# Rates and delay of the late modulation sums in a gated two-mixer layer

## The chip, the cores and the metric

The kernel runs on one core of a Trainium2 chip. Its time is the device time of one execution in microseconds. Three runs of the kernel before took 1473.76 to 1475.06 us, with a median of 1474.42 us. All arithmetic is float32: each large product is made of three TensorE products of a high and a low part.

## What is computed

One layer (DEPTH is 1) over 256 latent and 256 context tokens of width 2048. Six modulation vectors come from one conditioning vector. Two of them (sa, ca) shape the first norm; the other four (ga, cm, sm, gm) are not needed before the end of the mixers.

```python
mod = (jax.nn.silu(c) @ w_mod[l] + b_mod[l])[:, None, :]
sa, ca, ga, sm, cm, gm = jnp.split(mod, 6, axis=-1)
h = modulate(x, norm_attn_w[l], sa, ca)
p = h @ w_in[l]
q = axial_rope(rmsnorm(split_qk(p[..., Q_OFF:K_OFF]), q_norm_w[l]), row, col)
k = axial_rope(rmsnorm(split_qk(p[..., K_OFF:V_OFF]), k_norm_w[l]), row, col)
v = split_v(p[..., V_OFF:P_OFF])
mix = token_mixer(q, k_all, v_all, p[..., P_OFF:G_OFF], p[..., G_OFF:], lam, lam_init,
                  subln_w[l], pool_w[l], pool_scale[l], w_a_up[l], w_b_up[l], w_o[l])
x = x + ga * mix
x = x + gm * sq_relu_mlp(modulate(x, norm_mlp_w[l], sm, cm), w_ff1[l], w_ff2[l])
```

`token_mixer` is differential attention over 8 heads, a multi-scale pooling of a projection, sigmoid gates of both, and the projection `w_o`.

## The kernel before

The weights are streamed once, in chunks of 128 x 1024 floats (512 KB), in an order that the list `stream` fixes (L126 to L172). For each chunk SP issues the load into one of five `raw` buffers (L113 to L116), ACT casts it to the rounded high part `whi` (L233), and DVE subtracts to give the low part `wlo` (L234); there are three buffers of either. `load_next` does this, and `wchunk` runs two chunks ahead of their use. In the products of features by weights (`xstat`, L423 to L446) a chunk for two token tiles is eight matmuls with `whi` (L442, L443) and four with `wlo` (L445); for four token tiles it is twice that.

The stages are: the norms and the first keys and queries (ended at about 131 us), values of group 0, queries, keys and values of group 1, the pooling projection, the gates with their up projections (four groups of 24 chunks), `w_o` (four groups of eight chunks), and the feed-forward. Attention runs beside them: its generator is advanced by a count of matmuls. For one unit, TensorE makes two score tiles (L704), DVE their row maxima `mx` (L705), ACT the exponentials `e` (L709), DVE and ACT the difference of the two softmaxes (L712 to L715); later the result is transposed (`aTp`, `aT`). The keys and queries of group 1 are normed on DVE (`qraw`, L457 to L472) and transposed on TensorE (`qkT`, L477). PSUM has eight banks, all from one pool, so a new tile waits until the tile that held its bank was read.

The late modulation is the subject of the change. The products of silu(c) with the weights of ga, cm, sm and gm do not run on TensorE. For each of these vectors, in two halves of 1024 columns, `late_gen` (L599 to L632) clears an accumulator `macc` on POOL (L617), loads the bias into its first row from POOL's queue, and takes 16 chunks of weights: each is one more load into a `raw` buffer and one multiply-add `late_part` on DVE (L636), 128 in all. At the end of a half, `late_half` splits the two quarters of `macc` into `ah` (ACT, L259) and `al` (DVE, L260), and `late_sum` has TensorE add up the partitions with a tile of ones (`late`, L655 and L656), from where ACT or DVE writes the result. There are 16 such pairs of matmuls.

How often a late chunk is asked for is set by the rate in `stream`: each loaded weight chunk adds its rate to a credit, and each whole credit advances `late_gen` by one chunk. `later(n, fn)` puts a step off by n weight chunks: `tick` runs it when TensorE's program takes its n-th next chunk. A late part runs one chunk after its load where the rate is 1 or more, two where it is less; the product of a late sum stands three chunks behind the split. The order in which each engine gets its instructions is then fixed when the program is built, and an engine that waits for one holds all behind it.

One more place is touched without being edited. In `pooling` ACT copies the projection's two halves into `za` (L798), POOL adds up windows of them (L803), and DVE corrects the edges (L814, L816) and subtracts (L818).

The code of these functions:

Of the kernel before, what the change touches and what calls it, by code (L numbers as in the profile page):

```python
# [48 lines left out]
def layer(ctx: ExitStack, tc, a, out):  # L49
# [24 lines left out]
    def work(name, shape=None, dt=F32):  # L74
        return pool.tile(shape or [P, 512], dt, tag="w2", name=name, bufs=9)
# [19 lines left out]
    def later(n, fn):  # L95

        waiting.append([n, fn])
# [28 lines left out]
    def plan(name, *idx, rate=0.0):  # L126
        stream.append(((name,) + idx, rate))
# [12 lines left out]
            plan("w_k", 0, f // 2)  # L140
            plan("w_q", 0, f // 2)
    FIRST_LOADS = len(stream)
    for n, g, rate in (("w_v", 0, 0.75), ("w_q", 1, 1.0), ("w_k", 1, 1.5), ("w_v", 1, 1.5)):
        for ch in range(8):
            plan(n, g, ch, rate=0.0 if (n, g) == ("w_v", 1) and ch < 3 else rate)
    for g in range(4):
# [9 lines left out]
                    plan("pool_w", 2 if ch == 1 else 3)  # L156
    for g in range(4):
        for ch in range(8):
            plan("w_o", g, ch, rate=0.5 if g < 2 else 0.0)
            if ch % 4 == 0:  # L160
                plan("x", ch // 4, g)
    for b in range(9):
# [95 lines left out]
    def split(hi, lo, src):  # L258
        act.copy(hi, src)  # L259
        vec.tensor_sub(lo, src, hi.bitcast(F32))  # L260
# [377 lines left out]
    def late_split(acc, norm_w, o):  # L638
        for q in range(2):
            part = partial(late_half, q, acc, norm_w, o)  # L640
            if q == 0:
                part()
            else:
                later(2, part)
                parts.append(waiting[-1])

    def late_half(q, acc, norm_w, o):
        ah, al = work("ah", dt=F32R), work("al", dt=F32R)
        split(ah, al, acc[:, q * 512:q * 512 + 512])
        later(3, partial(late_sum, ah, al, norm_w[q] if norm_w else None, o[:, q * 512:q * 512 + 512]))  # L650

    def late_sum(ah, al, wr, o):

# [526 lines left out]
```

## Time and profile before

| | |
|---|---|
| median of the three runs | 1474.42 us (1473.76 to 1475.06) |
| the profiled execution | 1475.86 us |
| its span | 1474.0 us |
| TensorE busy | 1440.5 us, 98% |
| VectorE (DVE) busy | 1000.8 us, 68% |
| ScalarE (ACT) busy | 684.3 us, 46% |
| GpSimd (POOL) busy | 121.3 us, 8% |
| mean granted clock of TensorE | 0.99 |
| HBM traffic over the span | 235 GB/s |

The profile is of one execution. Its span goes from the first instruction to the last, 1.86 us less than the execution's time. In a row of the timeline stand the start and the length in us, the engine, the line of the kernel, the operation, what it writes and reads, the shape, and how many alike follow one another; in brackets how long the engine stood idle ahead of it, and what released it. In a row of the table of waits stand who waited for what, the us in total, how many times, and the longest. The clock is the share of full speed that TensorE was granted.

### The profile page before, as it was taken

What the parts mean: (1) busy time and instruction counts of PE and PEld (TensorE: products, weight loads), DVE (VectorE), ACT (ScalarE), POOL (GpSimd) and SP (SyncE); (2) the same over time, 40 slices, a digit from 0 to 9 for tenths busy, and PEclk for the clock granted to TensorE, in tenths of its full rate; (3) what the DMA queues carried; (4) which work ended last, traced back from release to release, by engine and by line L of the source; (5) the groups of instructions that cost most, each with busy time, mean ns of one, the idle gap of its engine ahead of it and who ended that gap; (6) DMA issues with size and microseconds to landing.
All of it is one profiled execution on the core that took longest, in us unless ns stands there. A gap on an engine that the chain in (4) does not pass through costs nothing.

```text
span 1474.0 us, 19772 instructions
## 1 busy us (share of the span) xinstructions
PE 1440.5 (98%) x7466; PEld 1186.7 (81%) x7466; DVE 1000.8 (68%) x1243; ACT 684.3 (46%) x929; POOL 121.3 (8%) x120
## 2 busy tenths in 40 slices
PE   4999999999999999999999999999999999999998
PEld 2667887778878888888878888888888888888887
DVE  4667786768887687778776755666665555555675
ACT  4334346466554444544444555445354454544442
POOL 0001110101400000000001000001000000000260
PEclk7999999999999999999999999999999999999999
DMA  9996685435788879798746776677765655566554
GB/s 380 401 407 224 203 287 167 143 114 165 234 284 294 301 279 301 278 330 294 252 146 222 233 237 226 234 239 240 238 230 186 193 192 189 191 193 191 186 195 141
DMA packets 97440, 347.85 MB, mean 236 GB/s; under 512 B 11073, under 2 KB 11713, under 8 KB 97345
## 3 DMA queue, kind: packets, MB, share of 16 engines
q1 hardware_dynamic: 96768, 345.51, 69.4%
q8 instruction: 58, 0.95, 0.3%
q0 software_dynamic: 576, 1.08, 0.2%
q14 instruction: 38, 0.30, 0.1%
HBM read 344.45 MB, written 2.10 MB: 235 GB/s over the span
## 4 chain that ended last, share of the span: by engine, by line
PE 88%; DVE 6%; ACT 2%; DMA 2%; issue 1%; POOL 0%; DVEq 0%; SPq 0%; ACTq 0%; POOLq 0%
PE f L1029 14%; PE f L443 8%; PE f L442 8%; PE f L445 8%; PE f L1032 7%; PE pg L443 3%; PE pg L442 3%; PE pg L445 3%; PE w_k L67 3%; PE wo L442 2%; PE wo L445 2%; PE wo L443 2%; PE pyy L445 2%; PE pyy L442 2%; PE pyy L443 2%; DVE wlo L234 2%
## 5 line engine op out<-in xcount | busy, mean ns | idle before, releaser
L234 DVE TENSOR_TENSOR wlo<-raw,whi 128x1024 fp32r<-128x1024 f32 (+1 forms) x433 | 538.4, 1245 | 349.1 <-ACT whi L233 324.1
L233 ACT CAST whi<-raw 128x1024 fp32r<-128x1024 f32 (+1 forms) x433 | 452.8, 1047 | 555.6 <-PE f L443 184.6
L1029 PE MATMUL f<-h,whi 128*128 128x512 f32 x896 | 224.3, 392 | 0.0
L443 PE MATMUL f<-whi,act 128*128 128x512 f32 x512 | 199.3, 389 | 0.0
L442 PE MATMUL f<-whi,act 128*128 128x512 f32 x512 | 199.2, 389 | 0.0
L1029 PEld LDWEIGHTS f<-h,whi 128*128 128x128 f32 x896 | 161.8, 189 | 29.6
L636 DVE SCALAR_TENSOR_TENSOR macc<-raw,sil,macc 128x1024 f32<-128x1024 f32 x128 | 165.0, 1289 | 3.3 <-issue 2.6
L445 PE MATMUL f<-wlo,act 128*128 128x512 f32 x512 | 136.8, 389 | 0.0
L1032 PEld LDWEIGHTS f<-h,wlo 128*128 128x128 f32 x896 | 122.2, 190 | 8.7
L1032 PE MATMUL f<-h,wlo 128*128 128x256 f32 x896 | 124.9, 282 | 0.0
L445 PEld LDWEIGHTS f<-wlo,act 128*128 128x128 f32 x512 | 96.1, 188 | 19.9
L443 PEld LDWEIGHTS f<-whi,act 128*128 128x128 f32 x512 | 96.2, 188 | 19.8
L442 PEld LDWEIGHTS f<-whi,act 128*128 128x128 f32 x512 | 96.2, 188 | 19.7
L442 PE MATMUL pg<-whi,hL 128*128 128x512 f32 x256 | 101.4, 396 | 0.0
L443 PE MATMUL pg<-whi,hL 128*128 128x512 f32 x256 | 100.6, 393 | 0.0
L1040 POOL TENSOR_TENSOR rsq<-relu 128x512 f32<-128x512 f32 x28 | 29.2, 1042 | 543.3 <-ACT relu L1039 523.0
L445 PE MATMUL pg<-wlo,hL 128*128 128x512 f32 x256 | 68.6, 390 | 0.0
L443 PEld LDWEIGHTS pg<-whi,hL 128*128 128x128 f32 x256 | 48.5, 189 | 10.4 <-issue 0.2
L442 PEld LDWEIGHTS pg<-whi,hL 128*128 128x128 f32 x256 | 48.5, 189 | 10.3 <-issue 0.2
L445 PEld LDWEIGHTS pg<-wlo,hL 128*128 128x128 f32 x256 | 48.3, 189 | 10.2
L617 POOL MEMSET macc<- 128x1024 f32 x8 | 7.6, 955 | 461.6 <-DVE al L260 357.1
L442 PE MATMUL wo<-whi,mix 128*128 128x512 f32 x116 | 45.2, 390 | 0.0
(263 smaller groups left out, 2083.4 us busy)
## 6 DMA issues: line engine op xcount, KB each, us to landing
raw<-in_w_ff_dram SPq DMA_DIRECT2D x240, 512.0 KB, 4.0
raw<-in_w_m_dram SPq DMA_DIRECT2D x64, 512.0 KB, 9.7
raw<-in_w_ga_dram SPq DMA_DIRECT2D x32, 512.0 KB, 4.6
raw<-in_w_cm_dram SPq DMA_DIRECT2D x32, 512.0 KB, 4.4
raw<-in_w_gb_in_dram SPq DMA_DIRECT2D x32, 512.0 KB, 4.7
raw<-in_w_ga_in_dram SPq DMA_DIRECT2D x32, 512.0 KB, 5.0
raw<-in_w_sm_dram SPq DMA_DIRECT2D x32, 512.0 KB, 4.8
raw<-in_w_o_dram SPq DMA_DIRECT2D x32, 512.0 KB, 5.2
```

The lines of the kernel that those rows point to most:

```text
L67: return (lambda *a, **k: pin(emit(*a, **k))) if self.flag[0] else emit
L233: act.copy(hi, raw)
L234: vec.tensor_sub(lo, raw, hi.bitcast(F32))
L442: pe.matmul(banks[t], tok(h, k, 0, tt), wt, start=k == 0, stop=False)
L443: pe.matmul(banks[t], tok(h, k, 1, tt), wt, start=False, stop=False)
L445: pe.matmul(banks[t], tok(h, k, 0, tt), wt, start=False, stop=k == 2 * nk - 1)
L617: gp.memset(acc, 0.0)
L636: pin(vec.scalar_tensor_tensor(acc, raw, sil[:, 0, k:k + 1], acc, ALU.mult, ALU.add))
L1029: pe.matmul(ps, hi[:, kk * P:kk * P + P], both(h2, k), start=k == 0, stop=False)
L1032: pe.matmul(ps[:, T:2 * T], lo[:, kk * P:kk * P + P], act_slice(h2, k, 0), start=False, stop=k == KT - 1)
L1040: gp.tensor_mul(sq, r, r)
```

## The change

Three numbers are edited. Of the late chunks, fewer are asked for during keys and values of group 1 (one per weight chunk rather than 1.5 in the keys, 0.75 rather than 1.5 in the last five chunks of the values), more during the first two groups of `w_o` (0.75 rather than 0.5). And the product of a late sum stands four chunks behind its split rather than three.

```diff
@@ -140,7 +140,7 @@
-    for n, g, rate in (("w_v", 0, 0.75), ("w_q", 1, 1.0), ("w_k", 1, 1.5), ("w_v", 1, 1.5)):
+    for n, g, rate in (("w_v", 0, 0.75), ("w_q", 1, 1.0), ("w_k", 1, 1.0), ("w_v", 1, 0.75)):
         for ch in range(8):
             plan(n, g, ch, rate=0.0 if (n, g) == ("w_v", 1) and ch < 3 else rate)
@@ -156,7 +156,7 @@
-            plan("w_o", g, ch, rate=0.5 if g < 2 else 0.0)
+            plan("w_o", g, ch, rate=0.75 if g < 2 else 0.0)
@@ -647,7 +647,7 @@
     def late_half(q, acc, norm_w, o):
         ah, al = work("ah", dt=F32R), work("al", dt=F32R)
         split(ah, al, acc[:, q * 512:q * 512 + 512])
-        later(3, partial(late_sum, ah, al, norm_w[q] if norm_w else None, o[:, q * 512:q * 512 + 512]))
+        later(4, partial(late_sum, ah, al, norm_w[q] if norm_w else None, o[:, q * 512:q * 512 + 512]))
```

All 128 late parts and all 16 pairs of matmuls remain. The late chunks of ga, cm and sm are reached later than before, and the four chunks of gm that were taken in `w_o` now come in the feed-forward, at its rate of 0.25. On TensorE nothing but the 16 pairs moves. On the other engines three places change that matter below.

The first is DVE in the values of group 1, where an attention unit is finished and the next one's maxima follow (at 268 to 277 us of the profile before). Before:

```order
L460 TENSOR_TENSOR qraw<-qraw,rq_y 128x512
L712 RECIPROCAL rs<-sm_2346 128x2
L636 SCALAR_TENSOR_TENSOR macc<-raw,sil,macc 128x1024
L472 TENSOR_TENSOR qraw<-qraw,wkt 128x512
L713 TENSOR_TENSOR rs<-rs,nlam 128x1
L234 TENSOR_TENSOR wlo<-raw,whi 128x1024
L715 SCALAR_TENSOR_TENSOR e<-e,rs 128x512
L636 SCALAR_TENSOR_TENSOR macc<-raw,sil,macc 128x1024 x2
L234 TENSOR_TENSOR wlo<-raw,whi 128x1024
L705 TENSOR_REDUCE mx<-sc 128x1 x2
```

DVE at the same place in the changed kernel:

```order
L460 TENSOR_TENSOR qraw<-qraw,rq_y 128x512
L712 RECIPROCAL rs<-sm_2334 128x2
L472 TENSOR_TENSOR qraw<-qraw,wkt 128x512
L713 TENSOR_TENSOR rs<-rs,nlam 128x1
L234 TENSOR_TENSOR wlo<-raw,whi 128x1024
L715 SCALAR_TENSOR_TENSOR e<-e,rs 128x512
L234 TENSOR_TENSOR wlo<-raw,whi 128x1024
L705 TENSOR_REDUCE mx<-sc 128x1 x2
```

The three late parts L636 no longer stand ahead of the maxima; the rest keeps its order.

The second is ACT in the first group of the gates, up to the sigmoids of the second gate (`pg_3988` and `pg_3989` are its banks; at 437 us of the profile before the casts `ah` stand here). Before:

```order
L833 ACTIVATE py<-pd,prm 128x256 x2
L233 CAST whi<-raw 128x1024
L259 CAST yb<-py 128x512
L233 CAST whi<-raw 128x1024 x8
L259 CAST ah<-macc 128x512 x2
L233 CAST whi<-raw 128x1024 x4
L853 ACTIVATE sgm<-pg_3988 128x512
```

ACT there in the changed kernel, where that bank is called `pg_3962`:

```order
L833 ACTIVATE py<-pd,prm 128x256 x2
L233 CAST whi<-raw 128x1024
L259 CAST yb<-py 128x512
L233 CAST whi<-raw 128x1024 x12
L853 ACTIVATE sgm<-pg_3962 128x512
```

The two casts of a late sum left this stretch; they stand behind the first group's gates now, in the second group.

The third is ACT from the last window of the pooling into the gates (384 to 394 us). Before:

```order
L259 CAST dh<-d 128x512
L233 CAST whi<-raw 128x512
L798 COPY za<-pin 128x256
L724 COPY aT<-aTp 128x4x128
L798 COPY za<-pin 128x256
L233 CAST whi<-raw 128x1024
L259 CAST oT<-osb 128x512
L233 CAST whi<-raw 128x1024 x2
L833 ACTIVATE py<-pd,prm 128x256 x2
```

ACT there in the changed kernel:

```order
L259 CAST dh<-d 128x512
L233 CAST whi<-raw 128x512
L724 COPY aT<-aTp 128x4x128
L259 CAST ah<-macc 128x512
L233 CAST whi<-raw 128x1024
L259 CAST oT<-osb 128x512
L798 COPY za<-pin 128x256 x2
L259 CAST ah<-macc 128x512
L233 CAST whi<-raw 128x1024 x2
L833 ACTIVATE py<-pd,prm 128x256 x2
```

The two casts of another late sum (of ga's second half) came into this stretch, and the two copies `za`, on which POOL's additions wait, moved behind one of them, a weight cast and the cast of `oT`.

## The prediction

> **What bounds the kernel now.** I read the busy table of the page first, then the table of waits for TensorE, then windows of the span, and last the timeline around each wait.
>
> ```profile
> PE 1440.5 (98%) x7466; PEld 1186.7 (81%) x7466; DVE 1000.8 (68%) x1243; ACT 684.3 (46%) x929; POOL 121.3 (8%) x120
> PE qkT L477 <- ACT e L709: 2.5, 1, 2.5
> ...
> PE late L655 <- ACT ah L259: 1.1, 1, 1.1
> PE late L656 <- DVE al L260: 0.8, 1, 0.8
> ```
>
> TensorE is busy for 98% of the span: the kernel is bound by its matmuls, and nothing but their count, their clock and TensorE's idle time sets the end. The change leaves the matmuls and their order as they are but for 16 pairs (L655 and L656) that stand elsewhere. So all it can win is idle time of TensorE and the slow clock that follows it. Behind the opening, the table of waits names only a handful of places; the three above are all that the change could touch.
>
> ```profile
> 250.00:300.00 50.00, 47.46 (x214) 36.61 (x214) 34.71 (x62) 24.08 (x48) 4.41 (x3) 0.97 0.43 136
> 400.00:450.00 50.00, 48.09 (x207) 38.91 (x206) 40.97 (x45) 24.13 (x29) 2.55 (x4) 0.97 0.88 292
> 750.00:800.00 50.00, 47.01 (x211) 37.51 (x210) 33.90 (x52) 21.21 (x31) 0.00 (x0) 0.97 0.50 158
> 450.00:500.00 50.00, 50.00 (x226) 41.46 (x226) 39.55 (x38) 22.01 (x24) 0.00 (x0) 1.00 0.87 295
> ```
>
> In these windows (width, busy time of PE, PEld, DVE, ACT, POOL, then granted clock, DMA share, GB/s) three of four lose two to three us of TensorE each and show a clock of 0.97; the fourth is what an undisturbed one looks like. The waits above lie in these three windows; I call them A (250 to 300), B (400 to 450) and C (750 to 800).
>
> **Stall A, second values group: about 4.0 us, and it goes.**
>
> ```profile
> 268.65 1.26 DVE L636 SCALAR_TENSOR_TENSOR macc<-raw,sil,macc 128x1024 f32<-128x1024 f32 x1
> 271.65 1.06 ACT L233 CAST whi<-raw 128x1024 fp32r<-128x1024 f32 x1 [0.25 <-DMA raw<-in_w_v_dram]
> 272.30 2.59 DVE L636 SCALAR_TENSOR_TENSOR macc<-raw,sil,macc 128x1024 f32<-128x1024 f32 x2
> 274.81 1.22 DVE L234 TENSOR_TENSOR wlo<-raw,whi 128x1024 fp32r<-128x1024 f32 x1
> 275.95 1.28 DVE L705 TENSOR_REDUCE mx<-sc 128x1 f32<-128x512 f32 x2
> 276.66 0.69 ACT L709 ACTIVATE e<-sc,mx 128x512 f32<-128x512 f32 x1 [3.96 <-DVE mx L705]
> 277.59 1.09 PE L477 MATMUL qkT<-prm,qraw 128*128 128x128 f32 x4 [2.54 <-ACT e L709]
> ```
>
> Read from the bottom: TensorE stood 2.54 us before qkT, for a bank whose score ACT had still to read; ACT's exponential waited 3.96 us for the row maxima; and these stood on DVE behind two late parts (L636, 2.59 us) and a weight split. Of the three L636 in these rows the change leaves none there, as its DVE order shows. Then the L234 of 274.81 is held only by its cast. If that cast comes as late as now (271.65 + 1.06 = 272.71), split (1.22), first maximum (half of 1.28) and exponential (0.69) end near 275.26; TensorE gets there at 277.59 - 2.54 = 275.05. So at worst about 0.2 to 0.5 us of waiting is left. At best the weights' load comes earlier as well, since no late loads stand ahead of it on SP, and nothing is left. I take nothing left.
>
> ```profile
> 441.13 0.63 PE L443 MATMUL pg<-whi,hL 128*128 128x512 f32 x1
> 441.56 0.63 PE L442 MATMUL pg<-whi,hL 128*128 128x512 f32 x1
> 445.24 0.40 PE L442 MATMUL pg<-whi,hL 128*128 128x512 f32 x1
> 445.47 0.40 PE L443 MATMUL pg<-whi,hL 128*128 128x512 f32 x1
> ```
>
> The second part of the price is the clock. Behind stall B matmuls start 0.43 us apart, later 0.23; the same stretch follows A. It holds some 3.4 us, in which about seven matmuls each cost 0.20 more: near 1.5 us. So A costs 2.54 + 1.5 = **4.0 us**. The Trainium skill, "TensorE: Matmul & The Clock Gate", Part 1 (The HAM clock gate), says that the clock falls to half after at least one idle window of 3.4 us and that the window runs free. Here the slow stretch has that length, but 2.54 us of idleness brought it on (for B, 1.91 in two pieces), so the trace doesn't bear out the threshold; by the rule the 3.0 us that I put down to the two slow stretches would not belong to these waits, and the time would come out by so much higher.
>
> **Stall B, gates: about 3.5 us, and it goes.**
>
> ```profile
> 437.58 1.05 ACT L233 CAST whi<-raw 128x1024 fp32r<-128x1024 f32 x1 [0.90 <-DMA raw<-in_w_ga_in_dram]
> 438.54 1.13 ACT L259 CAST ah<-macc 128x512 fp32r<-128x512 f32 x2
> 439.20 0.50 PE L655 MATMUL late<-ah,ones 128*128 128x512 f32 x1 [1.07 <-ACT ah L259]
> 440.55 0.50 PE L656 MATMUL late<-al,ones 128*128 128x512 f32 x1 [0.84 <-DVE al L260]
> ```
>
> TensorE waits twice in one late sum: for ah, whose cast stands on ACT behind a weight cast that waited for DMA, and for al, which follows ah on DVE: 1.07 + 0.84 + 1.6 of slow clock = **3.5 us**. With one chunk more between the casts and the product, a chunk being 8 matmuls at 0.23 and 4 at 0.22 (2.7 us), each of the waits would be covered. The half also ends elsewhere now: no ah stands on ACT in this stretch.
>
> The other 15 pairs move too. Each costs two matmuls wherever it stands, so nothing in sum. A pair adds a wait only if its ah or al is late: there are 2 us and more between the splits' and the products' places in the changed order, laid on the old times. The edits of the rates move whole parts: one L636 of DVE and one 512 KB load each.
>
> ```profile
> L636 DVE SCALAR_TENSOR_TENSOR macc<-raw,sil,macc 128x1024 f32<-128x1024 f32 x128 | 165.0, 1289 | 3.3 <-issue 2.6 <-DMA macc<-in_b_cm_dram 0.3 <-DVE rs L712 0.2
> L617 POOL MEMSET macc<- 128x1024 f32 x8 | 7.6, 955 | 461.6 <-DVE al L260 357.1 <-DVE lm L67 104.5
> ...
> macc<-in_b_cm_dram POOLq DMA_DIRECT2D x2, 4.0 KB, 3.2
> ```
>
> In the second keys 8 x 0.5 = 4 parts fewer are asked for, in the second values 5 x 0.75 = 3.75, in w_o 16 x 0.25 = 4 more, and the remaining 3.75 come in the feed-forward, at one per four chunks as now. All 128 stay, DVE's total too, so this costs nothing in itself. Each half's MEMSET (0.96) and bias load (3.2 to landing) on POOL's queue move with it, and at one place they matter, below.
>
> **Where it can be given back: from pooling into the gates.**
>
> ```profile
> 373.05 3.92 POOL L803 TENSOR_TENSOR za<-za 128x271 f32<-128x271 f32 x6 [0.87 <-ACT za L798]
> 384.61 0.37 ACT L798 COPY za<-pin 128x256 f32<-128x256 f32 x1
> 385.12 7.90 POOL L803 TENSOR_TENSOR za<-za 128x271 f32<-128x271 f32 x8 [1.52 <-ACT za L798]
> 391.74 0.62 ACT L259 CAST oT<-osb 128x512 fp32r<-128x512 f32 x1 [2.47 <-DVE osb L747]
> 393.05 0.17 DVE L816 TENSOR_TENSOR za<-za,prm 128x7 f32<-128x7 f32 x1 [0.83 <-POOL za L803]
> 399.35 1.07 PE L445 MATMUL pg<-wlo,hL 128*128 128x512 f32 x4
> ```
>
> Now ACT copies the last two za ahead of the cast of oT; in the change they stand behind an ah, a weight cast and oT, and oT waits for DVE's L747: they move from 384.61 to about 392. POOL's eight adds take 0.65 to 0.99 us each by these rows, so they end 5.2 to 7.9 us later, at 397.5 to 400. L816, in DVE's fixed order ahead of weight splits, waits for them, against 393.05 now. Behind it stands the wlo that TensorE uses at 399.35 (0.46 later with the late pair that the change puts ahead): with 1.22 us for the split that is 0.9 us to spare at the fast end, 1.5 us of waiting at the slow one. Behind the adds stand the next half's MEMSET and bias load, 4.2 us together, and for them the half's first L636 waits on DVE, at 402 to 404: the split behind it is due some 5.4 us after the one above (two chunks), at 405.7, with 1.2 for itself, so 0 to 1 us is lost there too. I take 0.3 for both, near the fast end, since DVE, waiting, doesn't slow POOL. The Trainium skill, "SBUF — State Buffer", section "SBUF: two separate sides", says that VectorE and GpSimd share one port pair as an exclusive lock; the rows agree (0.65 an add, and 0.99 beside DVE's work); by it the adds would take the fast price while DVE stands.
>
> ```profile
> 433.87 1.05 ACT L233 CAST whi<-raw 128x1024 fp32r<-128x1024 f32 x1 [3.09 <-DMA raw<-in_w_ga_in_dram]
> 435.25 0.39 PE L442 MATMUL pg<-whi,hL 128*128 128x512 f32 x1
> ```
>
> The five raw buffers are given back by such splits (an early release is an early load), so a block on DVE also delays loads. At 435.25 the weights were only 435.25 - 434.92 = 0.33 us ahead, and stall B is what refilled them. With B gone and DVE late, TensorE may wait for whi there: between nothing and 4 us, with a slow stretch 5.5. I take 0.3, near the low end, as the late load pattern (0.6 a chunk) is the same.
>
> **w_o, groups 0 and 1.**
>
> ```profile
> 180.00:205.00 25.00, 25.00 (x112) 20.71 (x111) 20.56 (x18) 10.03 (x11) 0.00 (x0) 1.00 0.96 333
> 660.00:706.00 46.00, 46.00 (x208) 38.17 (x207) 37.35 (x39) 23.29 (x29) 1.44 (x2) 1.00 0.87 300
> 674.03 1.05 ACT L233 CAST whi<-raw 128x1024 fp32r<-128x1024 f32 x1 [3.07 <-DMA raw<-in_w_o_dram]
> 676.99 0.39 PE L442 MATMUL wo<-whi,mix 128*128 128x512 f32 x1
> ```
>
> Sixteen w_o chunks, 8 late loads and 4 half-size x loads are 26 loads of 512 KB now and 30 in the change: 300 x 30/26 = 346 GB/s, over the 333 at a DMA share of 0.96 that the other row shows as reached. In 46 us that falls behind by 46 x 13/333 = 1.8 us at most. The weights are ahead by 1.9 us at the tightest place (cast ended 675.08, used 676.99), more later, so I take nothing; 1.8 + 1.5 is the upper end. DVE gets 4 x 1.29 = 5.2 us more on 37.35 of 46, which fits.
>
> **Sum.** Against the profiled execution (1475.86 us, its span 1474.0): -4.0 - 3.5 + 0.3 + 0.3 = -6.9. That run was 1.44 above the median of the three, 1474.42; the same sum on the median gives **1467.5 us**. Stall C stands in a part whose order is unchanged and stays; its slow stretch may come or not by where its waits fall in the free-running window: up to 1.5 us less, which sets the lower end at 1465.
>
> **Rivals.**
> 1. *The wait moves into the gates.* Block on L816, then weights short near 435: 3 to 5.5 us returned, 1470.5 to 1473. For it: 0.33 us ahead now. Against: behind the refill the supply keeps ahead at the same rate (450 to 500 has no idle time).
> 2. *w_o starves:* up to 3.3 us, 1468 to 1471.
> 3. *A doesn't go:* the moved parts aren't what holds the maxima, but the split with its late load; qkT still waits near 2 us and the slow stretch stays. 1474.42 - 3.5 = 1471. Against: the L636 of 272.30 alone is as long as the stall.
> 4. *Slower.* POOL's adds run at 0.99 or worse, L816 holds DVE until 400 or later, the loads behind it slip by the same, and TensorE meets missing weights repeatedly from 399 to 437, each time with idleness of 2 us or more and a slow stretch: three such are 3 x 3.5 = 10.5 us against 7.5 won, 1477.5. It decides from a block some 4 us longer than the spare, so that the loads never catch up in this group.
>
> **How the numbers follow.** Forecast 0.50 (1465 to 1469); the gates 0.20; w_o 0.07; A stays 0.10; slower 0.13. A measurement of this kernel tells about 0.2%, 2.9 us, from no change: faster is under 1471.5. From these, the forecast, w_o, half of the gates and half of A-stays are faster: 0.72; the other halves lie within, 0.15; slower 0.13. The range 1465 to 1474.5 takes in all but the last and a little of the gates.
>
> **What would show it.** In the changed profile the waits of TensorE should lack qkT on e and late on ah and al, and the windows 250 to 300 and 400 to 450 read 1.00 in the clock. C's waits should stand, some 7 us earlier. If L816 waits for POOL by several us and TensorE shows waits for whi or wlo between 395 and 440, the first or the fourth rival holds; if waits for w_o's whi stand near 670 to 700, the second. If qkT still waits for e while no L636 stands ahead of mx, the third does. I am wrong if the late pairs wait at their new places, or if slow stretches appear with no idle time ahead of them.

## The result and the profile after

The changed kernel took 1480.61 us (median of four runs, 1478.57 to 1483.19) against 1474.09 us (1473.63 to 1475.06): 1.0044 of the time before, with a 95% interval of 1.0027 to 1.006. It is slower by some 6.5 us, where 1467.5 was forecast and 1465 to 1474.5 given as the range. Run again beside other kernels (the run e11_after below) it took 1480.9 us, at a ratio of 1.0042 (1.0027 to 1.0058).

The profiled execution, 1478.57 us with a span of 1476.5, is the fastest of the four, so it shows the smaller part of the loss. The table of waits for TensorE in the changed kernel, in the columns of the one before:

```profile
PE wo L442 <- ACT whi L233: 2.6, 4, 0.8
...
PE pyy L442 <- ACT whi L233: 1.6, 1, 1.6
...
PE pg L445 <- DVE wlo L234: 1.1, 1, 1.1
...
PE h2T L944 <- DVE yt L67: 0.8, 1, 0.8
PE pyy L445 <- DVE wlo L234: 0.7, 1, 0.7
PE qkT L477 <- ACT e L709: 0.5, 1, 0.5
```

The qkT wait fell from 2.5 to 0.5 us, and no late pair waits any more. In their place stand waits for the weights, `whi` and `wlo`, in `w_o`, in the up projections (`pyy`) and in the gates (`pg`). The windows of the changed kernel (width, busy time of PE, PEld, DVE, ACT, POOL, then clock, DMA share, GB/s):

```profile
250.00:300.00 50.00, 49.47 (x231) 37.87 (x229) 32.37 (x62) 26.00 (x53) 4.45 (x3) 1.00 0.33 104
400.00:450.00 50.00, 47.68 (x212) 38.36 (x211) 39.95 (x43) 23.86 (x29) 1.16 (x2) 1.00 0.82 285
750.00:800.00 50.00, 46.26 (x214) 36.76 (x213) 34.83 (x55) 21.18 (x32) 0.00 (x0) 1.00 0.50 164
662.00:707.00 45.00, 42.32 (x181) 32.15 (x179) 35.27 (x36) 17.01 (x21) 0.00 (x0) 1.00 0.86 295
```

The clock is full in all of them: the three slow stretches are gone from this execution, C's too. Yet TensorE is now idle for a part of `w_o` (the last row), at 295 GB/s and a DMA share of 0.86, well under the 333 and 0.96 that the prediction took for the ceiling.

Where the time went is read best by stage, from the start of the first matmul of each. These are the rows of the kernel before:

```profile
317.54 0.68 PE L263 MATMUL pin<-hL,whi 128*128 128x256 f32 x1
385.98 0.58 PE L442 MATMUL pg<-whi,hL 128*128 128x512 f32 x1
662.49 0.39 PE L442 MATMUL wo<-whi,mix 128*128 128x512 f32 x1
752.58 0.50 PE L263 MATMUL f<-hi,h 128*128 128x512 f32 x1 [0.46 <-ACT h L67]
```

and those of the changed kernel (the last row of either is the first of the feed-forward):

```profile
313.89 0.68 PE L263 MATMUL pin<-hL,whi 128*128 128x256 f32 x1
381.15 0.58 PE L442 MATMUL pg<-whi,hL 128*128 128x512 f32 x1
660.19 0.39 PE L442 MATMUL wo<-whi,mix 128*128 128x512 f32 x1
755.73 0.50 PE L263 MATMUL f<-hi,h 128*128 128x512 f32 x1 [0.46 <-ACT h L67]
```

| stage, us | before | after | difference |
|---|---|---|---|
| start to pooling | 317.54 | 313.89 | -3.65 |
| pooling | 68.44 | 67.26 | -1.18 |
| gates | 276.51 | 279.04 | +2.53 |
| w_o | 90.09 | 95.54 | +5.45 |
| feed-forward to the end | 721.39 | 720.73 | -0.66 |
| span | 1473.97 | 1476.46 | +2.49 |

Two late pairs (0.46 us each) moved from the pooling into the gates, so without them the pooling gained 0.3 us and the gates lost 1.6, where stall B's 3.5 should have been won. `w_o` lost 5.5 us, where nothing was taken. The forecast was a span 6.9 us shorter, so the profile shows 9.4 us that it doesn't have: some 4.5 in the gates and 5.5 in `w_o`, less 0.6 elsewhere. Between the medians the difference is larger, 6.5 us, since the execution profiled before was 1.8 above its median and this one 2.0 under.

### The profile page after: what moved, and what is told of

Read it like the earlier page. It is cut to its first block, busy times and chain, and to the rows that moved or that the text cites. A ratio compares the mean times of both kernels' runs of the same rounds, so it can differ in the third digit from the quotient of the medians.

```text
span 1476.5 us, 19749 instructions
## 1 busy us (share of the span) xinstructions
PE 1439.7 (98%) x7466; PEld 1181.5 (80%) x7466; DVE 996.0 (67%) x1243; ACT 684.2 (46%) x929; POOL 120.8 (8%) x120
## 4 chain that ended last, share of the span: by engine, by line
PE 82%; DVE 7%; DMA 6%; ACT 2%; issue 2%; POOL 0%; DVEq 0%; ACTq 0%; SPq 0%; POOLq 0%
PE f L1029 14%; PE f L443 8%; PE f L442 8%; PE f L445 8%; PE f L1032 7%; PE w_k L67 3%; PE pg L445 3%; PE pg L442 2%; PE pg L443 2%; DVE wlo L234 2%; PE v L443 2%; PE v L442 2%; PE v L445 2%; DMA raw<-in_w_o_dram 2%; DVE macc L636 2%
## 5 line engine op out<-in xcount | busy, mean ns | idle before, releaser
L636 DVE SCALAR_TENSOR_TENSOR macc<-raw,sil,macc 128x1024 f32<-128x1024 f32 x128 | 164.6, 1286 | 8.5 <-issue 3.6
```

What stands on the lines that cost most here:

```text
L636: pin(vec.scalar_tensor_tensor(acc, raw, sil[:, 0, k:k + 1], acc, ALU.mult, ALU.add))
```

## The experiments

Two theories were set against each other and against the prediction's own terms. S: the five raw buffers bound the supply of weights, so that `w_o` at 0.75 overdraws it. P, formed after the fourth run: POOL's additions hold DVE at the head of the gates, which costs the weights' lead there (how long before its first matmul a chunk's cast has ended). Rivals are named with each run. Each profile is of one execution, and two executions of one kernel can differ by 4 us; so a stage's time is a size, and the verdicts go by the medians. The stage times given below are differences between first matmuls as above, each from the profile of that run. Ratios are to runs of the kernel before beside the same runs.

**The later product alone.**

```diff
-        later(3, partial(late_sum, ...
+        later(4, partial(late_sum, ...
```

> The kernel before with one edit: the late product four chunks behind its split rather than three; the rates are those of before. Theory S (supply): the five raw buffers barely carry the 1.6 loads a chunk of the gates, and a wait of TensorE there is also what gives the weights their lead back; so the wait for ah and al near 440 goes, but about as much comes back as waits for whi behind 435: 1471 to 1475, stall A unchanged at 2.5 us. Rival L (the later product itself costs, by holding ah and al one chunk longer): slower than before, 1476 or more, with waits at the late pairs or at what needs their buffers. The forecast's own view: 1470.5 to 1471.5, nothing coming back.

1473.91 us against 1474.49, ratio 0.9993 (0.9984 to 1.0002): no difference that can be measured, inside S's range and above the forecast's own view. In its profile the gates took 272.43 us, 4.1 less than before with the same six pairs in them, so stall B went with all that the forecast gave it and no wait came back there; S had the time, but not the place. The pooling took longer, 70.20 us (+1.8). The timeline shows where:

```profile
378.84 0.75 DVE L816 TENSOR_TENSOR za<-za,prm 128x3 f32<-128x3 f32 x2 [2.31 <-POOL za L803]
379.53 2.36 DVE L234 TENSOR_TENSOR wlo<-raw,whi 128x1024 fp32r<-128x1024 f32 x2
380.81 0.38 PE L265 MATMUL pin<-hL,wlo 128*128 128x256 f32 x1 [1.70 <-DVE wlo L234]
```

DVE stood 2.31 us in L816 for POOL, ahead of the split that TensorE then waited for. In the kernel before it stood there too, for 2.90 us, and TensorE waited only 0.5 us; so it isn't shown that the edit costs anything here. The later product is worth 4 us in the gates of this profile, and between the medians nothing of it can be seen.

**w_o at 0.75 alone.**

```diff
-            plan("w_o", g, ch, rate=0.5 if g < 2 else 0.0)
+            plan("w_o", g, ch, rate=0.75 if g < 2 else 0.0)
```

> The kernel before with one edit: w_o's first two groups ask for 0.75 late chunks per weight chunk rather than 0.5. S: TensorE waits for whi on w_o chunks as in the changed kernel (4.9 us lost between 674 and 707 there), here 2 to 5 us less what of the lead of before (2 to 5 us) covers it: 1475 to 1479. Rival L: no loss here, 1474. The forecast's estimate: 0 to 1.8 us plus a slow stretch, 1474 to 1477.5.

1482.46 us against 1474.49, ratio 1.0049 (1.0034 to 1.0065): slower by 8 us, more than either view gave. `w_o` took 100.05 us in its profile, 10 more than before. Beside waits for weights (1.4 and 1.2 us in sum) a late pair waits there:

```profile
PE late L655 <- ACT ah L259: 2.5, 1, 2.5
PE late L656 <- DVE al L260: 2.2, 2, 1.2
```

The wait for ah and one of 1.2 us for al lie in `w_o`, from 678 to 683 us, with a slow stretch behind them: from 662 to 707 us the granted clock was 0.96. These two waits and the slow clock (0.04 of 45 us) make some 5.5 of the 10 us, by estimate, and the changed kernel, with its later product, has none of them. So the denser loads alone cost more than the whole change does, but not by the same waits; the part left for missing weights is some 4.5 us, inside the 2 to 5 that S gave.

**The twelve late chunks of w_o over three groups.**

```diff
-            plan("w_o", g, ch, rate=0.75 if g < 2 else 0.0)
+            plan("w_o", g, ch, rate=0.5 if g < 3 else 0.0)
```

> The changed kernel with w_o's twelve late chunks spread over three groups at 0.5 rather than over two at 0.75. S: the waits for whi in w_o (4.9 us) all but vanish, those in the gates stay: 4 to 5 us under the changed kernel, 1475 to 1477. Rival L, and a rival by which w_o only shows a lag that comes from the gates: the waits stay within 1.5 us of what they were, 1479 to 1481.

1473.65 us against 1474.49, ratio 0.9996 (0.9987 to 1.0006): 7 us less than the changed kernel, by the density of the same loads alone, and a lower time than S gave (1475 to 1477). `w_o` took 91.47 us, 4.1 less, and the waits for `whi` between 674 and 707 us are gone; the gates' stayed (1.6 and 0.7 us at `pyy`), though the gates as a whole took 2.3 us less in this execution, without an edit there. So `w_o` doesn't only show a lag of the gates, and the rival falls; that all of the lag is made in `w_o` doesn't follow, as the runs e7_macc and e9_hold1wo below show.

**L816 kept behind L814** (both correct the edges of `za`; without it the program's scheduler puts L816 early).

```diff
-                vec.tensor_mul(s[:, T - n1:T], ...)
+                pin(vec.tensor_mul(s[:, T - n1:T], ...))
```

> The changed kernel with L816 kept in program order behind L814, so that DVE no longer stands for POOL's additions ahead of the weight splits (4.19 us at 392 in the changed kernel). S: SP's gap of 7.4 us without a load (386.9 to 394.3) shrinks, and the waits at 412 to 420 (3.0 us) and at 526 to 533 (1.7 us) go or shrink by 2 to 4.5 us together; w_o unchanged: 1476 to 1479. Rival: the gates' waits come from 1.6 loads a chunk alone, whatever DVE does at 392: same places, same sums, 1480 to 1481.

1480.1 us against 1474.49, ratio 1.0038 (1.0024 to 1.0051): like the changed kernel, and not S's 1476 to 1479. The waits at 415 to 420 stayed, as the rival had it. But the timeline shows that the block had only changed its name:

```profile
386.53 9.30 POOL L803 TENSOR_TENSOR za<-za 128x271 f32<-128x271 f32 x8 [4.53 <-ACT za L798]
...
389.56 1.91 SPq L115 DMA_DIRECT2D raw<-in_w_gb_in_dram  x2
...
395.77 0.95 POOL L617 MEMSET macc<- 128x1024 f32 x1
397.01 0.58 POOL L618 DMA_DIRECT2D macc<-in_b_cm_dram  x1 [0.29 <-PE late L656]
...
398.92 1.29 DVE L636 SCALAR_TENSOR_TENSOR macc<-raw,sil,macc 128x1024 f32<-128x1024 f32 x1 [6.76 <-DMA macc<-in_b_cm_dram]
400.12 2.35 DVE L234 TENSOR_TENSOR wlo<-raw,whi 128x1024 fp32r<-128x1024 f32 x2
400.23 0.33 SPq L115 DMA_DIRECT2D raw<-in_w_cm_dram  x1
```

DVE waits no longer in L816, but 6.76 us in the first late part of cm, whose accumulator POOL clears only behind its additions. SP issues no raw load from 391.5 to 400.2 us, since this part and the two splits behind it hold their buffers.

**POOL out of the way**: as in e4_pin816, and

```diff
-                gp.memset(acc, 0.0)
-                nc.gpsimd.dma_start(acc[0:1, :], a["b_" + name][half])
+                vec.memset(acc, 0.0)
+                nc.sync.dma_start(acc[0:1, :], a["b_" + name][half])
```

> Like e4_pin816, and the accumulator is cleared by DVE instead of POOL and its bias loaded from SP's queue, so that DVE waits for POOL neither with L816 nor with the half's first L636 (6.76 us near 399 in e4_pin816). Theory P: POOL's additions, by either way, take the weights' lead, and the waits at 415 to 420 (2.7 us) and at 531 come from that: they go, 2.5 to 3.5 us under e4_pin816, 1476.5 to 1478. Rival: the gates' demand of 1.6 loads a chunk takes the lead whatever POOL does: 1479.5 to 1481.

1472.36 us against 1473.93, ratio 0.999 (0.9981 to 1.0): 7.7 us under e4_pin816 (some 7 by the two ratios), more than P gave. The gates took 273.38 us instead of 277.55, without the waits at 415 and 531, and `w_o` 93.56 instead of 96.75: the lead carries over. (The first cast of `w_o` ended 5.0 us ahead of its matmul here, 1.4 in e4_pin816.) In its timeline POOL's additions took longer still, but cm's first part came at 394.34, beside them, and DVE stood only 0.63 us for POOL:

```profile
387.66 12.77 POOL L803 TENSOR_TENSOR za<-za 128x271 f32<-128x271 f32 x8 [4.54 <-ACT za L798]
...
394.34 1.65 DVE L636 SCALAR_TENSOR_TENSOR macc<-raw,sil,macc 128x1024 f32<-128x1024 f32 x1
...
399.77 0.69 DVE L814 TENSOR_TENSOR za<-za,prm 128x8 f32<-128x8 f32 x1 [0.63 <-POOL za L803]
```

**Late parts one chunk behind their load.**

```diff
-                    later(2 if credit_rate[0] < 1 else 1, partial(late_part, acc, raw, k))
+                    later(1, partial(late_part, acc, raw, k))
-                        later(2 if credit_rate[0] < 1 else 1, partial(late_split, acc, norm_w, o))
+                        later(1, partial(late_split, acc, norm_w, o))
```

> The changed kernel with late parts always one chunk behind their load, where rates under 1 gave two: a raw buffer of a late chunk comes back one chunk (2.7 us) earlier. S: what binds in w_o is the time that the five buffers are held (295 GB/s between 662 and 707 us, where 333 were seen in a stage with the short hold), so the waits for whi there shrink from 4.9 us to under 2: 1475 to 1478. Rival D (the DMA engines or the memory bind): the same loads, the same waits, 1479.5 to 1481.5. A second rival: parts so early wait on DVE for their own load and hold the splits behind them: slower than the changed kernel, with L636 waiting for DMA.

1471.3 us against 1473.93, ratio 0.9988 (0.998 to 0.9997), 9 us under the changed kernel with all its three edits in it, and a lower time than S gave (1475 to 1478): the gates gain as well. `w_o` took 90.09 us at 0.75, as long as before at 0.5: no wait is left there, 5.5 us less than in the changed kernel. The gates took 274.52, 4.5 less; their rate of 0.6 had the long hold too. The pooling took 2.2 more, where DVE stood 2.90 us in L816 for POOL. So neither the DMA engines nor the memory bind: they carried the same loads in time. What differs is how long a buffer is held. In the changed kernel a load and the part that releases its buffer, from the timelines of SP and DVE:

```profile
692.07 0.33 SPq L115 DMA_DIRECT2D raw<-in_w_sm_dram  x1
...
701.76 1.28 DVE L636 SCALAR_TENSOR_TENSOR macc<-raw,sil,macc 128x1024 f32<-128x1024 f32 x1
```

That is 11.0 us; a load and its part at the same place with the short hold, 9.0 us:

```profile
684.30 0.33 SPq L115 DMA_DIRECT2D raw<-in_w_sm_dram  x1
...
691.99 1.28 DVE L636 SCALAR_TENSOR_TENSOR macc<-raw,sil,macc 128x1024 f32<-128x1024 f32 x1
```

Paired so for all loads issued in `w_o`'s first two groups, nine late loads are held for 11.8 us in the changed kernel and nine for 9.5 with the short hold; 16 weight loads for 7.6 us in the changed one. A weight chunk and 0.75 of a late one need 7.6 + 0.75 x 11.8 = 16.5 us of a buffer, over five buffers 3.3 us, where TensorE needs 90.09/32 = 2.8 a chunk: 16 chunks fall behind by some 8 us, of which the lead on arrival (the first cast ended 1.7 us ahead of its matmul) covers 2; the stage lost 5.5. With the short hold it is 7.6 + 0.75 x 9.5 = 14.7, or 2.9 us a chunk, which the lead (5.1 us there) carries. This is an estimate from mean holds.

**The short hold in w_o alone** (the rate written as 0.7500001, so that the rule can tell it).

```diff
-                    later(2 if credit_rate[0] < 1 else 1, ...
+                    later(1 if credit_rate[0] >= 1 or 0.75 < credit_rate[0] < 0.76 else 2, ...
```

> The changed kernel with one edit: in w_o alone late parts run one chunk behind their load rather than two; the rate there stays 0.75, the gates stay as they are. Theory S: the hold of the raw buffers is what makes w_o starve, so its waits for whi (4.9 us lost between 674 and 707 us in the changed kernel) go or fall under 1.5, and the gates' waits (412 to 420, 526 to 533) stay: 3.5 to 6 us under the changed kernel, 1474.5 to 1477. Rival: the gain of e6_hold1 came from the gates alone, w_o only inherits its lead: 1479 to 1481.

1476.88 us against 1475.39, ratio 1.0012 (1.0002 to 1.0021): 4.0 us under the changed kernel beside it, inside what S gave. But its profile, of the slowest of its twelve executions, has `w_o` at 94.27 us, 4.2 over the 90.09 of a stage without waits for weights, not under 1.5. The hold in `w_o` is therefore a part of that loss. The rest fits weights that come into `w_o` with hardly any lead: the gates took 279.10 us here, and the first cast of `w_o` ended 0.5 us ahead of its matmul, against 5.1 in e6_hold1 and 5.0 in e7_macc. No run varied this lead alone.

**Of the change, only the values' rate and the later product.**

```diff
-("w_k", 1, 1.0), ("w_v", 1, 0.75)
+("w_k", 1, 1.5), ("w_v", 1, 0.75)
-            plan("w_o", g, ch, rate=0.75 if g < 2 else 0.0)
+            plan("w_o", g, ch, rate=0.5 if g < 2 else 0.0)
```

> The changed kernel with the keys' rate at 1.5 and w_o's at 0.5 as before: of the change there remain the values' rate (0.75) and the product one chunk later. As many late chunks are asked for ahead of the feed-forward as in the changed kernel (103). Theory S (raw buffers bound the supply, and w_o at 0.75 overdraws it): no L636 ahead of the maxima near 272, so stall A goes (3.5 us); ga's second half ends in the pooling as before, so POOL's additions hold nobody in the gates; w_o as before. Against the kernel with the later product alone (1473.9) that is 3.5 less: 1469 to 1472. Rival R (whatever is won early is given back by the next wait, so that the sum stays): 1473 to 1475.

1471.17 us against 1473.93, ratio 0.9986 (0.9977 to 0.9994). Stall A is gone (the stretch to the pooling is 3.5 us shorter from the values of group 1 on), and `w_o` took 90.09 us. The gates took 275.65, with waits of 1.0, 0.7 and 0.6 us, which S had not given. The first two stand at the same two matmuls as in the changed kernel (416.09 and 418.90 us), though at the head of the gates POOL held DVE for only 0.83 us in L816, and no late part waited there for its accumulator. So 3.2 of the 4.1 us that the later product won in e1_sum4's gates came back without POOL's block there: the block is not the only thing that empties the lead, and what the other is was not tested. R, by which every gain is given back, falls.

**The best of them.** e8_all is e7_macc with `w_o` as in e3_spread; e10_best adds the short hold.

> Like e7_macc, and w_o's twelve late chunks spread over three groups at 0.5 as in e3_spread. S and P together: e3_spread (1473.65) less the gates' 2.5 to 3.5 us: 1470 to 1471.5. If the gates' waits are not POOL's: 1473 to 1474. Rival R: 1473 to 1475 as well, but with the gates' waits gone and others in their place.

> e8_all with late parts one chunk behind their load everywhere. S: the short hold adds lead in the gates and in w_o, where e8_all has only two waits left (0.6 us near 439, 1.1 us near 737): 1467 to 1468.5. Rival: nothing is left to win by supply, and parts run early hold DVE for their load, as the wait for wlo near 374 in e6_hold1 (2.3 us) looks: 1469 to 1471.

e8_all took 1468.77 us against 1473.93, ratio 0.9964 (0.9951 to 0.9976); e10_best 1469.42 against 1475.39, ratio 0.9963 (0.9949 to 0.9977). Both are faster than the kernel before and the changed one, and alike: with the supply repaired the short hold has nothing left to win, which is the rival's time in e10_best. Its reason isn't borne out: the wait near 374 in e6_hold1 was DVE's for POOL in L816, not a part's for its load. e8_all came out under all the times given for it.

**The changed kernel once more.**

> The changed kernel once more, beside the other two on one chip, as what they are compared with: 1478.5 to 1483 as in its first four runs, with waits in w_o and in the gates in every profile.

1480.9 us, with waits for `whi` in `w_o` of 3.1 us, and the same ones in the gates. What makes two executions of it differ by 4 us isn't settled: the profiles are of single executions.

## Why the prediction was wrong

**Stall A: right.** From the values of group 1 to the pooling (62.01 us before, 58.53 after) the kernel became 3.5 us shorter, against 4.0 forecast; 0.5 us of the wait was left, as in the worst case given. **Stall B: right in itself**, 4.1 us in the gates of e1_sum4's profile against 3.5, though that run's median shows no gain. **The late pairs: right**, none waits.

**The clock.** The slow stretches behind A and B went with them, and C's with the new phase. C brought 0.7 us instead of up to 1.5, because TensorE, faster there, now meets `yt` 0.8 us too early: the row h2T <- DVE yt above is new, with DVE's order unchanged. Nothing of the loss is clock. The waits of the changed kernel, none over 1.6 us and scattered, brought on no slow stretch; in e2_wo75 the 2.5 and 1.2 us of one late pair did. Neither is as long as the idle window of about 3.4 us that the Trainium skill, "TensorE: Matmul & The Clock Gate", Part 1, asks for.

**w_o: the step that failed first.** "I take nothing; 1.8 + 1.5 is the upper end" went by 333 GB/s as what the DMA can carry, read from a stage where late parts release their buffer after one chunk. In `w_o` they release it after two, and five buffers then carried 295 to 301 GB/s (the changed kernel twice and e4_pin816, 662 to 707 us, all with waits). The stage lost 5.5 us in the profile where the prediction had put 0. Of these, 4.1 come back with the lower density (e3_spread) and all with the short hold (e6_hold1, which comes with a fuller lead); so density, hold and the lead on arrival set it, not the DMA. It was mis-sized by asking which resource had moved the most bytes, not how long a buffer is out.

**The gates: the mechanism was right, the size wrong.** The prediction had the block: the `za` copies later, POOL's additions late, DVE held in L816, and cm's first part behind POOL's MEMSET. It took 0.3 us for it, and 0.3 for the loads behind it. In the changed kernel it looks like this:

```profile
386.18 6.72 POOL L803 TENSOR_TENSOR za<-za 128x271 f32<-128x271 f32 x8 [4.53 <-ACT za L798]
386.88 0.33 SPq L115 DMA_DIRECT2D raw<-in_w_cm_dram  x1
392.25 0.86 DVE L816 TENSOR_TENSOR za<-za,prm 128x7 f32<-128x7 f32 x2 [4.19 <-POOL za L803]
394.30 1.47 SPq L115 DMA_DIRECT2D raw<-in_w_gb_in_dram  x2
397.85 1.28 DVE L636 SCALAR_TENSOR_TENSOR macc<-raw,sil,macc 128x1024 f32<-128x1024 f32 x1 [1.43 <-issue]
```

The changed kernel reaches the gates 4.83 us earlier, so POOL's start at 386.18 is 391.0 on the old times, 1 us ahead of the 392 that the prediction took. L816 ran at 397.1 on these, close to the fast end that it gave (397.5), and no split was late at its own place. The price came as loads: for 7.4 us, from 386.9 to 394.3, SP issued none. TensorE met that at 417:

```profile
417.11 0.50 PE L442 MATMUL pyy<-whi,yb 128*128 128x512 f32 x1 [1.57 <-ACT whi L233]
419.93 1.20 PE L445 MATMUL pyy<-wlo,yb 128*128 128x512 f32 x4 [0.71 <-DVE wlo L234]
```

and went on to the next wait near 533 (1.14 us) and into `w_o` with a lead of 1.7 us. e7_macc shows the size: 4.2 us in the gates and 3.2 in `w_o` come back when POOL hardly holds anybody. The prediction priced the block by the matmul that stood next, and the loads behind it, which it named, near the low end of "between nothing and 4 us"; the three waits make 3.4. In e5_combo waits came at the same place without the block, so how much of the loss is the block's alone stays open.

**The rivals.** The first and the second came about together, with some 5 us each in the profile (the gates lost 1.6 where 3.5 should have been won, `w_o` 5.5); the prediction gave each its own chance and neither their sum, and that sum, over the 7.5 us won, is the other sign. The fourth had the block right, but not how it would reach its price: no wait came with a slow stretch, and `w_o` was as large a part.

## What to carry to other kernels

Where a ring of buffers feeds the bound engine, the ceiling is the number of buffers over the time that each is out, from issue to release, weighed by what shares the ring; a rate seen in a stage with another hold doesn't carry over. An engine's wait ahead of instructions that release such buffers is to be priced in loads not issued, and looked for tens of microseconds later. And when two thin places stand in line, their chances go together: lead that is lost in the first is missing in the second, as e4_pin816 and e7_macc show (96.75 and 93.56 us of the same `w_o`).

## What was not expected of the hardware

Eight of POOL's additions (128 x 271 floats) took 6.72 us while DVE stood for 4.19 of them, 7.90 in the kernel before, 9.30 in e4_pin816 and 12.77 in e7_macc, where DVE worked beside them for most of the time: 0.84 to 1.60 us each. That agrees in kind with the Trainium skill, "SBUF — State Buffer", section "SBUF: two separate sides", on the port pair that VectorE and GpSimd share as an exclusive lock. DVE's side shows it too: an L636 beside the additions in e7_macc took 1.65 us, where the mean is 1.29. So POOL's work beside a busy DVE took up to 2.5 times the 0.65 us each of the prediction's row, and it cost next to nothing once hardly anybody waited for it.
